# The first gate group of the linear attention by seven products of quarters, and the input's sums written behind the queries' projection

## The chip, the cores and the metric

The kernel runs on one core of a Trainium2 chip. The metric is the device time of one execution in microseconds. Five engines work side by side, each through its own queue in order: TensorE (PE; its weight loads are shown as PEld), VectorE (DVE), ScalarE (ACT), GpSimd (POOL) and SyncE (SP). Weights and activations come from memory by DMA transfers that these queues issue.

## The reference

Two layers. Each normalises the input, projects it, runs three branches beside each other, multiplies each by its own gate path, and sends all of them through one output projection into the residual:

```python
h = _rmsnorm(x, norm_g)
proj = h @ w_in            # 512 tokens x 2048 by 2048 x 7696
(cv_h, cv_b, cv_c, cv_g, sb_q, sb_k, sb_v, sb_g,
 gl_q, gl_k, gl_v, gl_g, gl_lr) = split(proj)
y_conv = short_conv(cv_h, cv_b, cv_c) * silu(cv_g)
y_sb   = stick_breaking(rmsnorm(q), rmsnorm(k), v) * silu(sb_g)
y_gla  = rmsnorm(gla(gl_q, gl_k, gl_v, decay(gl_lr))) * silu(gl_g)
return x + concat(y_conv, y_sb, y_gla) @ w_out
```

The change touches `gl_g`, the gate of the gated linear attention (GLA). It has 512 columns and is projected in two groups of 256, "gla gate 0" and "gla gate 1".

## The kernel before

**Numbers.** Every 32-bit factor is split into a high and a low half of 16 bits. A product is then three matmuls: high by high, high by low, low by high.

**Groups.** The weights are cut into groups of 256 output columns, listed in the order of the work (`spec`). In each layer these are gla v 0, gla v 1, gla q, gla k, gla gate 0, gla gate 1, conv h, c, g and b 0, then four rounds of v, g, q and k of the stick-breaking attention, conv h, c, g and b 1, and eight groups of the output. `weights()` (L536) starts a group: it fetches the group after the next into one of two staging buffers, on POOL's queue, and hooks the preparation of the next group behind a matmul of this one.

**Preparing a group.** ACT squares the two halves of the weights with a running sum (`wmax`, L383). POOL adds these sums over the partitions (L399), and DVE turns the sum into a scale, a power of two (`wscale`, L402 to L417). Then the split: a classic group has ACT write two high halves of 128x2048 (`whi`, L454) and DVE two low halves (`wlo`, L461). They lie in a pool of three pairs of buffers.

**Projecting a group, the classic way.** `project_cols` (L701 to L703) multiplies both halves of the group's columns by all 16 slices of the depth: 2 x 16 x 3 = 96 matmuls with 512 tokens as the moving side.

**Projecting a group by seven products.** Groups named in `QUICK_IN` go through `project_quick`. The matrix product is cut into quarters and made of seven products of quarters instead of eight, by a scheme that shares sums. The weights' part is in `wsums` (L508, L527 to L532): one sum is made by a transfer that POOL issues and that accumulates in place (L386), three by DVE, and seven quarters of 128x1024 are split on ACT (L507) and DVE (L508). They take all three pairs of buffers and one pair more. The input's part is `xsums` (L734, L742): DVE forms sums of quarters of the normalised input once in each layer, and ACT and DVE split them; all the layer's groups in `QUICK_IN` share them as `insums`. The results of the products are combined from PSUM by ACT copies (L808, L812, L815) and five DVE operations (L809 to L821). PSUM has three banks for projections; either way a group takes two.

**What sets the order.** Outside the first stretch, which is ordered by hand, a planner orders each engine's queue: it simulates the program with its own costs and takes, among the instructions that are ready, the one that comes first in the source. Preparation of weights stands ahead of other work (`high_priority`). So the place of a line in the source is its rank, not its time.

**Around the change.** After gla v 0 and v 1 the queries and keys are projected, and each result is scaled: DVE finds the largest value (L1007), POOL reduces it over the partitions (L183), DVE makes a scale of it (L189 to L1014), and ACT copies the result out of PSUM with that scale (L1016). Then `xsums` is called, and the two gates are projected by `project_gate` with a logarithmic sigmoid on ACT and DVE (L874 to L884). DVE and ACT meanwhile prepare the GLA's attention, level by level (L1037 to L1086), whose small matmuls (L1051) fall between the projections.

Of the kernel before, what the change touches and what calls it, by code (L numbers as in the profile page):

```python
# [27 lines left out]


QUICK = ((3, 4, 5, 6), (3, 4, 5, 6))  # L30
QUICK_IN = ("conv c 1", "gla gate 1", "conv g 1", "conv g 0", "conv c 0") + tuple(f"{n} {j}" for n in "gqk" for j in range(4))

AHEAD = (8, 17, 21)

# [9 lines left out]
def hybrid_trunk(ctx, tc, x, norm_g, w_in, conv_w, conv_b, sb_qn_g, sb_kn_g,  # L44
# [33 lines left out]
    def wk(shape, tag, bufs=None, dt=F32):  # L78
        return work.tile(shape, dt, tag=tag, name=nm(tag), bufs=bufs)

    def newbig(tag, shape, dt, side):
        return big.tile(shape, dt, tag=f"big{side}", name=nm(tag))
# [236 lines left out]
    def spec(name, l, src, cols):  # L319
        if name in (QUICK[l] if src is w_out else QUICK_IN):  # L320
            quick.add(len(specs))
        specs.append((l, src, cols))
        names.append(str(name))
# [361 lines left out]
    for l in range(depth):  # L685
# [45 lines left out]
        def sums_of(src, parts, room):  # L731

            def do(f, *a):
                steps.append(f(*a))  # L734

            for t in range(2):
                (h11, h12), (h21, h22), (l11, l12), (l21, l22) = (
                    (a[:, q, 0::2, :], a[:, q, 1::2, :]) for a in src for q in (t, t + 2))

                def put(n, a):  # L740
                    hi, lo = (p_[:, t] for p_ in parts[n])
                    S.activation(hi, a, AF.Copy)  # L742
                    do(V.tensor_tensor, lo, a, hi, ALU.subtract)

                e, g, f = room(t)
                do(V.tensor_tensor, f, h22, l22, ALU.add)
                do(V.tensor_tensor, e, h21, f, ALU.subtract)
                do(V.tensor_tensor, e, e, l21, ALU.add)
                do(V.tensor_tensor, g, h11, e, ALU.subtract)
                do(V.tensor_tensor, g, g, l11, ALU.add)  # L750
                put(0, g)
                do(V.tensor_tensor, f, g, f, ALU.subtract)
                put(3, f)
                put(1, e)
                do(V.tensor_tensor, e, h12, g, ALU.subtract)
                do(V.tensor_tensor, e, e, l12, ALU.add)
                put(2, e)
            return parts
# [11 lines left out]
        def xsums():  # L770

            parts = []
            for _ in range(2):
                a = newbig("s", [P, 4, 2, HK, P], F16, 1 - l)
                parts.extend([a[:, 2 * n], a[:, 2 * n + 1]] for n in range(2))
            return sums_of((xh, xl), parts, lambda t: [wk([P, HK, P], tag) for tag in ("zw", "zw", "g")])
# [73 lines left out]
        def project_gate(mx=None, logistic=False, room=None):  # L850

            g = []

            def dst():
                g.append(room or wk([P, 2, seq], "g"))
                return g[0]

            ps, u = project(True, dst)
            quick_ = bool(g)
            g = dst() if not quick_ else g[0]  # L860
            top = sm(2, "gtop2") if mx is not None else None
            for c in range(2):
                y = g[:, c, :]
                if logistic:
                    a = wk([P, seq], "ga") if quick_ else y
                    tables.append(S.activation(a, ps[c], AF.Sigmoid, scale=u))
                    for b in tables[-9:-1]:
                        order(tables[-1], b)
                    if mx is None:
                        V.scalar_tensor_tensor(y, ps[c], u, a, ALU.mult, ALU.mult)  # L870
                    else:
                        V.tensor_tensor_reduce(y, ps[c], a, u, 0.28, ALU.mult, ALU.max, top[:, c:c + 1])
                    continue
                S.activation(y, ps[c], AF.Copy, scale=u)  # L874
                a = wk([P, seq], "ga")
                S.activation(a, y, AF.Abs)
                S.activation(a, a, AF.Exp, scale=-1.0)
                S.activation(a, a, AF.Ln, bias=1.0)
                V.scalar_tensor_tensor(a, y, 0.0, a, ALU.min, ALU.subtract)
                tables.append(S.activation(a, a, AF.Exp))  # L880
                if mx is None:
                    V.tensor_tensor(y, y, a, ALU.mult)
                else:
                    V.tensor_tensor_reduce(y, y, a, 1.0, 0.28, ALU.mult, ALU.max, top[:, c:c + 1])  # L884
            if mx is not None:
                V.tensor_tensor(mx, top[:, :1], top[:, 1:], ALU.max)
            return g, u
# [114 lines left out]
        for tag in ("qT", "kT"):  # L1002
# [15 lines left out]
            un = sm(1, tag + "un")  # L1018
            V.tensor_tensor(un, p2, u, ALU.mult)
            qku.append(un)  # L1020
        insums = xsums()
        gq, gk = qk
        att_u = sm(1, "attu")
        V.tensor_scalar(att_u, qku[0], qku[1], 0.125, ALU.mult, ALU.mult)
# [30 lines left out]
        for p in range(2):  # L1055
# [53 lines left out]
            for two, bias in ((0, (nT[:, p, 0:1], None, nT[:, p, 2:3], None)),  # L1109
                              (1, (nT01[:, p:p + 1], nT[:, p, 1:2], None, nT[:, p, 2:3]))):  # L1110
                e = wk([P, 2, 256], "e")
                n = [0, 0]
# [201 lines left out]
        for j in range(4):  # L1314
# [14 lines left out]
            g, _ = project_gate(bm[:, 1:2], True)  # L1329
# [144 lines left out]
```

## Time and profile before

| | us |
|---|---|
| median of 3 runs | 1646.34 |
| lowest and highest run | 1645.41, 1650.85 |
| the profiled execution | 1652.09 |
| its span, from the first to the last instruction | 1650.3 |

The profile shows one execution, whose time is 1.8 us more than its span. A row of the timeline begins with the start and the length in us; a row of groups ends with the total, the mean of one in ns, and the idle time of the engine just before, with what ended it. In the first layer gla gate 0 runs on PE from 117.6 to 138.3, gla gate 1 from 138.3 to 158, conv h 0 from 158 to 182, and conv c 0 and conv g 0 from 182 to 224. In the second layer gate 0 begins at 925.1 and gate 1 at 946.5.

### The profile page before, as it was taken

What the parts mean: (1) busy time and instruction counts of PE and PEld (TensorE: products, weight loads), DVE (VectorE), ACT (ScalarE), POOL (GpSimd) and SP (SyncE); (2) the same over time, 40 slices, a digit from 0 to 9 for tenths busy, and PEclk for the clock granted to TensorE, in tenths of its full rate; (3) what the DMA queues carried; (4) which work ended last, traced back from release to release, by engine and by line L of the source; (5) the groups of instructions that cost most, each with busy time, mean ns of one, the idle gap of its engine ahead of it and who ended that gap; (6) DMA issues with size and microseconds to landing.
All of it is one profiled execution on the core that took longest, in us unless ns stands there. A gap on an engine that the chain in (4) does not pass through costs nothing.

```text
span 1650.3 us, 41605 instructions
## 1 busy us (share of the span) xinstructions
PE 1624.0 (98%) x17914; PEld 1342.5 (81%) x17914; DVE 1418.1 (86%) x2377; ACT 1184.7 (72%) x1743; POOL 265.8 (16%) x298
## 2 busy tenths in 40 slices
PE   8999999999999999999999999999999999999999
PEld 6746668989999967799986468689898989668998
DVE  7977989989898978898699689898898889888893
ACT  7667887877777776756766687787777768666571
POOL 0121011111112121111112011221121111211110
PEclk9999999999999999999999999999999999999999
DMA  7144334486768687544633344445776886894441
GB/s 259 54 146 127 73 113 100 116 161 149 166 148 167 148 167 207 161 154 150 204 110 116 103 116 112 132 94 137 152 157 153 151 163 152 165 189 157 154 155 53
DMA packets 193913, 234.90 MB, mean 142 GB/s; under 512 B 90226, under 2 KB 154044, under 8 KB 193216
## 3 DMA queue, kind: packets, MB, share of 16 engines
q0 software_dynamic: 76992, 177.22, 40.5%
q1 hardware_dynamic: 107728, 45.56, 14.5%
q10 hardware_dynamic: 9008, 9.45, 1.7%
q8 instruction: 140, 2.29, 0.6%
q14 instruction: 45, 0.37, 0.1%
HBM read 179.65 MB, written 14.68 MB: 118 GB/s over the span
## 4 chain that ended last, share of the span: by engine, by line
PE 37%; DVE 6%; DMA 4%; ACT 2%; issue 1%; POOL 0%; SPq 0%; DVEq 0%; ACTq 0%; POOLq 0%
PE psp L796 10%; PE psp L793 6%; PE psp L843 5%; PE psp L712 3%; PE psp L714 3%; PE psp L713 3%; PE psp L701 2%; PE psp L702 2%; PE psp L703 2%; DMA st<-in_w_in_dram 2%; DVE wl L508 1%; DMA m<-mixd 1%; DMA th<-za 1%; DVE za L1280 1%; DMA kT<-raw 1%
## 5 line engine op out<-in xcount | busy, mean ns | idle before, releaser
L507 ACT ACTIVATE wh<-st,ws 128x1024 f16<-128x1024 f32 x252 | 280.8, 1145 | 174.5 <-DVE st L527 92.0
L508 DVE SCALAR_TENSOR_TENSOR wl<-st,ws,wh 128x1024 f16<-128x1024 f32 x252 | 316.7, 1278 | 31.1 <-ACT wh L507 31.0
L383 ACT ACTIVATE junk<-st 128x2048 uint8<-128x2048 f32 x150 | 285.4, 1903 | 17.9 <-DMA st<-in_w_in_dram 8.8
L793 PE MATMUL psp<-s,wh 128*128 128x256 f16 x1152 | 195.6, 273 | 0.0
L793 PEld LDWEIGHTS <-wh 128*128 128x128 f16 x1728 | 168.3, 98 | 21.5 <-issue 1.3
L796 PE MATMUL psp<-wh,s 128*128 128x128 f16 x2048 | 176.9, 219 | 1.9 <-issue 1.9
L714 PE MATMUL psp<-wh,m 128*128 128x256 f16 x640 | 174.5, 273 | 1.2 <-DVE m L1189 1.2
L712 PE MATMUL psp<-wh,m 128*128 128x256 f16 x640 | 174.5, 273 | 0.2 <-issue 0.2
L796 PEld LDWEIGHTS <-s 128*128 128x128 f16 x3072 | 172.9, 98 | 2.0 <-issue 2.0
L713 PE MATMUL psp<-wl,m 128*128 128x256 f16 x640 | 174.5, 273 | 0.0
L796 PE MATMUL psp<-wl,s 128*128 128x128 f16 x1024 | 173.2, 219 | 0.0
L461 DVE SCALAR_TENSOR_TENSOR wl<-st,ws,wh 128x2048 f16<-128x2048 f32 x68 | 158.9, 2346 | 14.6 <-ACT wh L454 13.8
L454 ACT ACTIVATE wh<-st,ws 128x2048 f16<-128x2048 f32 x66 | 130.5, 1995 | 40.7 <-DVE ws L415 22.6
L362 POOL DMA_DIRECT2D st<-in_w_in_dram x114 | 109.8, 1029 | 297.8 <-DVE w7l L508 110.7
L793 PE MATMUL psp<-s,wl 128*128 128x256 f16 x576 | 156.7, 273 | 0.0
L796 PEld LDWEIGHTS <-m 128*128 128x128 f16 x2304 | 131.1, 98 | 2.7 <-issue 2.2
L399 POOL PARTITION_ALL_REDUCE wgm<-wm x75 | 55.5, 740 | 482.5 <-ACT junk L383 469.4
L386 POOL DMA_DIRECT2D st<-st x34 | 54.0, 1589 | 307.2 <-ACT junk L383 266.8
L793 PEld LDWEIGHTS <-wl 128*128 128x128 f16 x864 | 84.5, 98 | 13.4 <-issue 3.4
L796 PE MATMUL psp<-wh,m 128*128 128x128 f16 x1024 | 91.5, 219 | 0.4 <-DVE kT L809 0.4
L796 PE MATMUL psp<-wl,m 128*128 128x128 f16 x512 | 87.5, 219 | 0.0
L703 PEld LDWEIGHTS <-wl 128*128 128x128 f16 x448 | 43.8, 98 | 53.6 <-DVE wl L461 2.3
(442 smaller groups left out, 4199.8 us busy)
## 6 DMA issues: line engine op xcount, KB each, us to landing
st<-in_w_in_dram POOLq DMA_DIRECT2D x114, 1024.0 KB, 8.3
st<-in_w_out_dram POOLq DMA_DIRECT2D x32, 1024.0 KB, 8.5
st<-st POOLq DMA_DIRECT2D x34, 512.0 KB, 6.8
st<-in_w_in_dram SPq DMA_DIRECT2D x6, 1024.0 KB, 12.0
mixd<-g POOLq DMA_DIRECT2D x20, 256.0 KB, 7.9
x<-in_x_dram SPq DMA_DIRECT2D x4, 1024.0 KB, 4.9
qT<-in_x_dram ACTq DMA_DIRECT2D x8, 512.0 KB, 6.2
qT<-xs ACTq DMA_DIRECT2D x8, 512.0 KB, 4.0
```

The lines of the kernel that those rows point to most:

```text
L362: load = queue.dma_start(s_, src[l, h * HK * P:(h + 1) * HK * P, c0:c0 + GW].rearrange("(k p) n -> p k n", p=P), max_dma_last_dim=1024)
L383: sq = S.activation(junk(HK * GW).rearrange("p (k n) -> p k n", k=part.shape[1]), part, AF.Square, accum_out=peak[i][:, h:h + 1])
L454: hi = S.activation(wh[:, :, :GW], staged[i][h], AF.Copy, scale=scales[i])
L461: V.scalar_tensor_tensor(wl[:, :, :GW], staged[i][h], scales[i], wh[:, :, :GW], ALU.mult, ALU.subtract)
L507: hi = S.activation(h_, b, AF.Copy, scale=sc)
L508: V.scalar_tensor_tensor(l_, b, sc, h_, ALU.mult, ALU.subtract)
L712: T.matmul(o, ah[:, t, k, :], wh[:, kk, :n], start=st_, stop=False, skip_group_check=True)
L713: T.matmul(o, ah[:, t, k, :], wl[:, kk, :n], start=False, stop=False, skip_group_check=True)
L714: return T.matmul(o, al[:, t, k, :], wh[:, kk, :n], start=False, stop=en, skip_group_check=True)
L793: mm = T.matmul(o, w[q_][:, kk, :], a[p_][:, :, kk, :], start=st_, stop=en, skip_group_check=True)
L796: mm = T.matmul(o[:, t * P:(t + 1) * P], a[p_][:, t, kk, :], w[q_][:, kk, :], start=st_, stop=en, skip_group_check=True)
L843: mm = T.matmul(o[:, :n], a_[:, t, k, :], w[k // HK][part][:, k % HK, :n], start=i == 0 and k == 0, stop=i == 2 and k == KT - 1)
```

## The change

"gla gate 0" joins the groups that are projected by seven products, in both layers. The call of `xsums` moves from behind the loop over queries and keys into it, behind the queries.

```diff
-QUICK_IN = ("conv c 1", "gla gate 1", "conv g 1", "conv g 0", "conv c 0") + tuple(f"{n} {j}" for n in "gqk" for j in range(4))
+QUICK_IN = ("conv c 1", "gla gate 0", "gla gate 1", "conv g 1", "conv g 0", "conv c 0") + tuple(f"{n} {j}" for n in "gqk" for j in range(4))
...
             un = sm(1, tag + "un")
             V.tensor_tensor(un, p2, u, ALU.mult)
             qku.append(un)
-        insums = xsums()
+            if tag == "qT":
+                insums = xsums()
         gq, gk = qk
```

## The prediction

> **What bounds the kernel now.** I read the page first, for the engines' shares.
>
> ```profile
> span 1650.3 us, 41605 instructions
> PE 1624.0 (98%) x17914; PEld 1342.5 (81%) x17914; DVE 1418.1 (86%) x2377; ACT 1184.7 (72%) x1743; POOL 265.8 (16%) x298
> ```
>
> PE is nearly always busy, but ends of matmuls are modelled, so the 98% alone says little. The waits of PE come next; columns are what waited, for whom, the total in us, how often, the longest.
>
> ```profile
> PE psp L793 <- DVE zw L809: 3.1, 2, 1.6
> PE psp L793 <- DVE w7l L508: 2.0, 2, 1.1
> PE psp L703 <- DVE wl L461: 1.3, 1, 1.3
> ```
>
> Only a few microseconds in 1650 are waits for operands. So PE's own stream sets the end, and an instruction taken off it counts in full as long as nobody else becomes late. The three rows show who would: each time DVE, twice in the same place (L809, once in each layer).
>
> Third, the windows, cut at the groups of the GLA stage: first layer's end of q and k (94 to 117), gate 0, gate 1, conv h 0, conv c 0 and conv g 0, conv b 0; then the second layer's k, gate 0, gate 1, conv h 0.
>
> ```profile
> 94.00:117.00 23.00, 23.00 (x108) 10.42 (x107) 18.07 (x45) 18.22 (x23) 3.58 (x5) 1.00 0.28 92
> 117.00:138.00 21.00, 21.00 (x99) 9.53 (x98) 11.74 (x30) 10.53 (x17) 3.36 (x5) 1.00 0.51 126
> 138.00:158.00 20.00, 20.00 (x220) 17.20 (x218) 16.87 (x29) 15.11 (x19) 3.99 (x5) 1.00 0.33 110
> 158.00:182.00 24.00, 23.95 (x228) 11.38 (x225) 21.07 (x48) 20.43 (x41) 2.00 (x2) 1.00 0.44 108
> 182.00:224.00 42.00, 40.38 (x388) 34.56 (x387) 40.98 (x68) 33.27 (x46) 6.28 (x7) 1.00 0.43 113
> 224.00:248.00 24.00, 24.00 (x123) 11.95 (x122) 19.52 (x36) 22.40 (x32) 5.63 (x7) 1.00 0.36 111
> 904.00:925.00 21.00, 21.00 (x99) 9.57 (x98) 14.72 (x35) 16.04 (x21) 2.49 (x4) 1.00 0.31 101
> 925.00:946.00 21.00, 21.00 (x99) 9.52 (x98) 11.51 (x30) 10.32 (x17) 4.11 (x5) 1.00 0.52 126
> 946.00:966.00 20.00, 20.00 (x214) 17.11 (x213) 16.75 (x28) 15.11 (x19) 3.99 (x5) 1.00 0.31 99
> 966.00:990.00 24.00, 24.00 (x244) 11.50 (x235) 21.41 (x49) 20.86 (x41) 1.98 (x2) 1.00 0.46 116
> ```
>
> After the window come its length, then PE, PEld, DVE, ACT and POOL busy, and the granted clock, 1.00 throughout. In gate 0, PE is full while DVE is busy 11.74 of 21 us and ACT 10.53: the group has slack on both. That is the stage the change touches. From 182 to 224 it is the other way round: DVE is busy 40.98 of 42 us, and the first L809 wait lies there.
>
> **PE: seven products for the classic 96 matmuls.** These are the timeline's first and last matmul of gate 0, then gate 1's first, the first of its second product, and the last of its first four products.
>
> ```profile
> 117.58 0.38 PE L701 MATMUL psp<-x,wh 128*128 128x512 f16 x1
> 138.08 0.38 PE L703 MATMUL psp<-x,wl 128*128 128x512 f16 x1
> 138.30 0.27 PE L793 MATMUL psp<-x,wh 128*128 128x256 f16 x1
> 140.92 0.27 PE L793 MATMUL psp<-s,wh 128*128 128x256 f16 x1
> 148.67 0.27 PE L793 MATMUL psp<-s,wh 128*128 128x256 f16 x1
> ```
>
> Gate 0 issues 2 column halves x 16 slices x 3 = 96 matmuls of 512 columns, starting 20.50 us apart over 95 steps: 0.216 each, 20.7 us. The new form has 7 products x 8 slices x 3 = 168 matmuls of 256 columns. Gate 1's first 96 of them start 10.37 us apart over 95 steps: 0.109 each, so 168 take 18.3. PE saves 2.4 us a layer, 4.8 in all.
>
> A rule speaks against this. The Trainium skill, "TensorE: Matmul & The Clock Gate", section "Back-to-back issue gap", gives a sustained spacing of 131 ns for 512 columns and 81 ns for 128. Estimated from that page, 256 columns would take some 98 ns, so 96 wide matmuls 12.6 us and 168 narrow ones 16.4, a loss of 3.8 a layer, or some 1654 us for the kernel. The trace disagrees: it has 216 and 109 ns for these very groups.
>
> **DVE, ACT and POOL: what is added.** The rows are groups by line and form; the number after "busy" is the mean in ns.
>
> ```profile
> L508 DVE SCALAR_TENSOR_TENSOR wl<-st,ws,wh 128x1024 f16<-128x1024 f32 x252 | 316.7, 1278 | 31.1 <-ACT wh L507 31.0
> L507 ACT ACTIVATE wh<-st,ws 128x1024 f16<-128x1024 f32 x252 | 280.8, 1145 | 174.5 <-DVE st L527 92.0 <-PE psp L796 19.4 <-PE psp L714 14.5
> L461 DVE SCALAR_TENSOR_TENSOR wl<-st,ws,wh 128x2048 f16<-128x2048 f32 x68 | 158.9, 2346 | 14.6 <-ACT wh L454 13.8
> L454 ACT ACTIVATE wh<-st,ws 128x2048 f16<-128x2048 f32 x66 | 130.5, 1995 | 40.7 <-DVE ws L415 22.6 <-PE psp L702 9.3 <-PE psp L714 4.2
> L527 DVE TENSOR_TENSOR st<-st 128x1024 f32<-128x1024 f32 x34 | 41.6, 1223 | 0.7
> L816 DVE TENSOR_TENSOR g<-psp,g 128x256 f32<-128x256 f32 x20 | 8.4, 418 | 11.3 <-ACT g L815 11.3
> L808 ACT ACTIVATE g<-psp 128x256 f32<-128x256 f32 x20 | 7.9, 397 | 5.8 <-PE psp L796 5.8
> L386 POOL DMA_DIRECT2D st<-st x34 | 54.0, 1589 | 307.2 <-ACT junk L383 266.8 <-ACT th L1043 20.4 <-ACT own L1103 20.0
> ```
>
> DVE a layer: two low halves go (2 x 2.35 = 4.7); seven low quarters (7 x 1.28 = 8.9), three sums of quarters (3 x 1.22 = 3.7) and five combinations of results (5 x 0.42 = 2.1) come, together +10.0. ACT: 7 x 1.15 + 3 x 0.40 - 2 x 2.00 = +5.2. POOL issues one more accumulating transfer, 1.6 us. The squares stay as many.
>
> What hides it: from 94 to 182 DVE is idle 4.9 + 9.3 + 3.1 + 2.9 = 20.2 us in the first layer (in the second, from 904 to 990, 6.3 + 9.5 + 3.3 + 2.6 = 21.7). Less the 2.4 that PE takes off the stretch, some 18 us stand against 10.0. ACT has at least as much. It fits if at least 10 of the 18 can be used. That is why I take most of the gain, but not all, since two places are tight.
>
> The first lies inside gate 0. Gate 1 today is the precedent: a group of quarters behind a classic one. ACT's and DVE's timelines there:
>
> ```profile
> 132.02 1.15 ACT L507 ACTIVATE wh<-st,ws 128x1024 f16<-128x1024 f32 x1 [5.06 <-PE psp L702]
> 138.81 2.48 DVE L508 SCALAR_TENSOR_TENSOR wl<-st,ws,wh 128x1024 f16<-128x1024 f32 x2 [0.35 <-ACT wh L507]
> ```
>
> The second split waits for the classic group's buffer until 132.02, the sums follow, and the second product's low part is ready halfway through the pair, about 140.1, for a product that starts at 140.92: 0.8 us to spare. In the new gate 0 the same chain runs beside the keys' own scaling:
>
> ```profile
> 117.98 1.63 POOL L386 DMA_DIRECT2D st<-st  x1
> 119.89 0.47 POOL L183 PARTITION_ALL_REDUCE gagm<-gamx  x1
> 121.77 1.25 ACT L1016 ACTIVATE kT<-psp,gas 128x512 f32<-128x512 f32 x2
> ```
>
> The keys' two results leave PSUM from 121.77, so the first bank is free at 122.4; the third product (117.58 + 2 x 2.62 = 122.8) needs it. Before, the second column half (24 x 0.216 = 5.2 later) needed it at the same moment. New splits on DVE and ACT queue around the steps of that chain. One DVE quarter and one sum in front (2.5 us) would cost PE 2.1 us; hidden, nothing. A gain is excluded, since no wait is there today. I take 0.5 a layer, near the precedent, which waits nowhere, and keep 0 to 2.1.
>
> The second is conv c 0, where PE waits 1.6 us for L809 in each layer. If DVE gets there no earlier than now, this wait grows by the 2.4 saved; if its slack carries the extra, not at all. I take 0.5 a layer, nearer to nothing because of the 18 against 10, and keep 0 to 2.4.
>
> **Fetches behind gate 0.** The staging buffer comes free when the seventh quarter is split, about 123 (117.6 plus four DVE quarters or sums of 1.25), not at 116, so conv h 0's weights start some 7 us later.
>
> ```profile
> 116.20 1.78 POOL L362 DMA_DIRECT2D st<-in_w_in_dram  x2 [16.67 <-DVE wl L461]
> 135.24 1.89 ACT L383 ACTIVATE junk<-st 128x2048 uint8<-128x2048 f32 x1
> 157.99 0.39 PE L701 MATMUL psp<-x,wh 128*128 128x512 f16 x1
> ```
>
> Their squares now run at 135.24, and PE needs them at 157.99. That cover of over 20 us hides the delay: nothing. Queued behind that fetch on POOL are the accumulate and the reductions of the rows above. If the order stayed and POOL waited for the buffer at 123, the keys' bank would come 5 us late; the planner sees that release, so I give this to the slower rival.
>
> **The move of the sums.** Their last low parts in either layer:
>
> ```profile
> 84.77 1.22 DVE L734 TENSOR_TENSOR s<-zw,s 128x1024 f16<-128x1024 f32 x1
> 895.22 1.22 DVE L734 TENSOR_TENSOR s<-zw,s 128x1024 f16<-128x1024 f32 x1
> 925.14 0.38 PE L701 MATMUL psp<-m,wh 128*128 128x512 f16 x1
> ```
>
> Sums end at 86.0 and 896.4, before gate 0 begins at 117.6 and 925.1. They already run as early filler, so a source line behind q instead of k moves them at most a little. From the waits, it can at best remove the one L461 wait (1.3) and at worst put two more sums (2.4) ahead of q's low half: I take 0.
>
> **The sum.** 2 x (-2.4 + 0.5 + 0.5) = -2.8. The profiled execution took 1652.09 us with its span of 1650.3, so it would take 1649.3; the runs' median is 1646.34, 5.75 below the profiled one, and becomes 1643.5.
>
> **The rivals.**
>
> *The wait only moves.* PE is early, DVE is not, and conv c 0 takes it back: 2 x (-2.4 + 2.4) = 0, with up to 1.0 inside gate 0: about 1647. For it speaks that both L809 waits already stand there; against it, DVE's idle before. 0.22.
>
> *DVE becomes the bound: slower.* Less than 10 us of its idle can be used, because its splits wait for buffers and the rest for its queue. It decides once over 2.4 us a layer doesn't fit: then conv c 0 waits longer than PE has saved. With half not fitting, 2 x (5.0 - 2.4) = +5.2; with all, 2 x (10.0 - 2.4) = +15.2; POOL's 5 us above gives as much as the first. I put it at 1653. The windows up to 224 speak for it, the idle 4.5 us at 224 to 248 against its going further. The Trainium skill, "Perfetto Trace Analysis", section "Identifying the Most-Contended Engine", takes weight loads and not matmuls for PE's occupancy: by that rule DVE, at 86% against PEld's 81%, is the engine to spare, and this rival holds. The waits of PE speak for the opposite. 0.20.
>
> *The new order also takes waits away.* With both L809 waits (3.1) and the L461 wait gone, and nothing lost: -4.8 - 4.4, 1637. Nothing in the change aims at that. 0.10.
>
> *The change does not do what it says*: gate 0 would still run at L701 to L703. The name is matched as gate 1's is, so 0.01.
>
> **How the numbers follow.** A measurement here can tell about 0.3%, 4.9 us: faster is below 1641.4, slower above 1651.3. The forecast has 0.47; its own range goes from the whole 4.8 kept, 1641.5, to nothing kept, 1646.3. Its lower end touches the border, so that 0.06 of it falls below; with the 0.10 of the rival in which waits go, faster is 0.16. The slower rival lies beyond 1651.3 in nearly all its chance, with a little of the wait that moves: slower 0.22. The rest, 0.62, is the same. Leaving out a tenth at either end gives 1639 to 1654.
>
> **What would show it.** Right: L793 has 336 matmuls more and L701 to L703 192 fewer; gate 0 takes about 18.3 us plus whatever small matmuls fall into it; DVE is 20 us busier in all; L809's waits stay below 5 us. Wrong: PE idle inside gate 0 above 1 us a layer, POOL waiting at L362 in front of the keys' L183, or L809 waits above 7 us. Wrong in the other direction: sums that end elsewhere than before gate 0 with PE waits of other lines gone.

## The result, and the profile after

The changed kernel takes 1649.99 us (median of 21 runs, 1645.96 to 1663.39) against 1646.45 for the kernel before (21 runs, 1645.16 to 1650.85): a ratio of 1.0027, with a 95% interval of 1.0016 to 1.0038. That is 3.5 us slower, where 2.8 us faster was forecast. The profiled execution took 1649.7 us.

The head of the page: span and instructions, then busy time, share and instructions of each engine.

```profile
span 1647.9 us, 41922 instructions
PE 1619.9 (98%) x18058; PEld 1357.2 (82%) x18058; DVE 1434.2 (87%) x2403; ACT 1192.8 (72%) x1759; POOL 273.0 (17%) x300
```

TensorE has 144 matmuls more, as 336 narrow ones in place of 192 wide ones must give. Its time went where the second view shows, the waits of PE:

```profile
PE psp L793 <- DVE g L809: 6.0, 2, 3.0
...
PE psp L796 <- DVE raw L816: 2.8, 2, 1.4
PE psp L793 <- DVE w7l L508: 1.9, 2, 1.1
...
PE psp L703 <- DVE wl L461: 1.3, 1, 1.3
```

The two waits for `zw` in conv c 0 are gone. In their place stand two of 3.0 us for `g` at the same line, now inside gate 0, and two of 1.4 us at L816, in the stick-breaking groups some 200 us later. The windows of gate 0 (first layer), conv c 0 and conv g 0, and gate 0 (second layer) show the price, in PE's column and in the granted clock, the third figure from the end:

```profile
117.00:139.00 22.00, 18.99 (x159) 15.93 (x157) 16.75 (x36) 13.04 (x18) 2.65 (x5) 0.92 0.52 120
...
182.00:224.00 42.00, 42.00 (x395) 35.45 (x394) 38.79 (x62) 34.46 (x45) 7.06 (x8) 1.00 0.38 98
...
925.00:948.00 23.00, 20.01 (x164) 16.39 (x162) 17.83 (x36) 14.12 (x18) 3.73 (x5) 0.93 0.50 115
```

Before, PE was full in gate 0 and lost 1.6 us in conv c 0; now it is the other way round, with 3.0 us lost, and the clock falls as well. PE's timeline around the wait shows both:

```profile
122.63 0.27 PE L793 MATMUL psp<-s,wh 128*128 128x256 f16 x1
125.89 0.37 PE L793 MATMUL psp<-x,wh 128*128 128x256 f16 x1 [2.99 <-DVE g L809]
126.06 0.42 PE L793 MATMUL psp<-x,wl 128*128 128x256 f16 x1
126.27 0.63 PE L793 MATMUL psp<-x,wh 128*128 128x256 f16 x2
126.70 0.42 PE L793 MATMUL psp<-x,wl 128*128 128x256 f16 x1
...
128.82 0.38 PE L793 MATMUL psp<-x,wh 128*128 128x256 f16 x2
129.04 0.27 PE L793 MATMUL psp<-x,wl 128*128 128x256 f16 x1
```

Two products are done at 122.90; the next begins at 125.89, and its matmuls start 0.21 us apart until 128.8, twice the 0.109 they take from then on. What holds it up is in DVE's timeline of the same stretch:

```profile
117.51 0.69 DVE L1007 TENSOR_REDUCE gamx<-psp 128x1 f32<-128x512 f32 x1 [0.41 <-PE psp L703]
118.80 0.16 DVE L1010 TENSOR_TENSOR gam<-gagm 128x1 f32<-128x1 f32 x1 [0.60 <-POOL gagm L183]
118.88 1.28 DVE L508 SCALAR_TENSOR_TENSOR wl<-st,ws,wh 128x1024 f16<-128x1024 f32 x1
120.08 0.15 DVE L189 TENSOR_SCALAR gapc<-gam 128x1 f32<-128x1 f32 x1
120.14 1.27 DVE L508 SCALAR_TENSOR_TENSOR wl<-st,ws,wh 128x1024 f16<-128x1024 f32 x1
121.33 0.14 DVE L190 TENSOR_SCALAR gapc<-gapc 128x1 int32<-128x1 int32 x1
...
121.46 1.28 DVE L508 SCALAR_TENSOR_TENSOR wl<-st,ws,wh 128x1024 f16<-128x1024 f32 x1
122.66 0.15 DVE L191 TENSOR_SCALAR kTp<-gapc 128x1 f32<-128x1 f32 x1
...
122.78 1.28 DVE L508 SCALAR_TENSOR_TENSOR wl<-st,ws,wh 128x1024 f16<-128x1024 f32 x1
123.97 1.22 DVE L532 TENSOR_TENSOR st<-st 128x1024 f32<-128x1024 f32 x1
125.11 0.16 DVE L1014 RECIPROCAL gas<-kTp 128x1 f32<-128x1 f32 x1
...
125.42 0.42 DVE L809 TENSOR_TENSOR g<-psp,g 128x256 f32<-128x256 f32 x1
```

The small rows L1007 to L1014 are the keys' scaling (the keys' chain, below), each step waiting for the one ahead. Between them stand four low quarters and a sum of gate 0's own weights, 4 x 1.28 + 1.22 = 6.3 us. Two of the quarters and the sum serve the fifth and later products, which start no earlier than 127.8 if PE runs on (117.31 + 4 x 2.62). Both ways on for PE are shut by them: the second pair of results needs the keys' bank, which ACT empties only after L1014, and the fifth product, which the planner put third in TensorE's queue, writes on in a bank that L809 must read first.

**The account**, per layer, in the profiled execution: PE saves 2.4. The wait costs 3.0. From its end at 125.89 to 128.80 the clock is at half, so 2.91 us do the work of 1.46 (second layer 2.80 and 1.40). Conv c 0 gives back 1.6, L816 takes 1.4. Together 2 x (-2.4 + 3.0 + 1.4 - 1.6 + 1.4) = +3.6.

This lists prices at five places; that it comes near the 3.5 between the medians proves nothing. The two traces can be laid side by side from a small matmul ahead of the gates (L965) to one of the stick-breaking attention far behind them (L1264, one line lower after the change). The first layer's stretch goes from 85.84 to 370.46 before and from 85.57 to 371.13 after, 0.9 us longer; the second layer's from 893.85 to 1179.17 and from 894.67 to 1180.14, 0.15 longer. So the profiled pair shows a loss of 1.1 us there, not 3.6. Part of the difference is that only the kernel before waits for the keys' transfers in these stretches (L1264, 0.45 and 0.93 us); the rest was not traced. Over the whole span the pair even stands the other way round, 1650.3 before and 1647.9 after, because that execution of the kernel before lost time much later (waits of PE of 1.91 us at 1301.86 and 1.20 at 1488.51). The medians' other 2.4 us no profile shows. Falls of the clock in other runs would account for some of it: the five runs of the changed kernel with a mean clock of 0.999 have a median of 1647.89, 1.4 above that of the kernel before.

### The profile page after: what moved, and what is told of

It is laid out like the page before. It is cut to its first block, busy times and chain, and to the rows that moved or that the text cites. A ratio compares the mean times of both kernels' runs of the same rounds, so it can differ in the third digit from the quotient of the medians.

```text
span 1647.9 us, 41922 instructions
## 1 busy us (share of the span) xinstructions
PE 1619.9 (98%) x18058; PEld 1357.2 (82%) x18058; DVE 1434.2 (87%) x2403; ACT 1192.8 (72%) x1759; POOL 273.0 (17%) x300
## 5 line engine op out<-in xcount | busy, mean ns | idle before, releaser
L507 ACT ACTIVATE wh<-st,ws 128x1024 f16<-128x1024 f32 x264 | 294.6, 1145 | 176.8 <-DVE st L527 90.5
L508 DVE SCALAR_TENSOR_TENSOR wl<-st,ws,wh 128x1024 f16<-128x1024 f32 x264 | 332.8, 1279 | 36.5 <-ACT wh L507 36.2
L793 PE MATMUL psp<-s,wh 128*128 128x256 f16 x1280 | 217.6, 273 | 0.0
L793 PEld LDWEIGHTS <-wh 128*128 128x128 f16 x1920 | 188.8, 98 | 25.5 <-issue 2.7
L793 PE MATMUL psp<-s,wl 128*128 128x256 f16 x640 | 174.3, 273 | 0.0
L461 DVE SCALAR_TENSOR_TENSOR wl<-st,ws,wh 128x2048 f16<-128x2048 f32 x64 | 149.5, 2347 | 12.1 <-ACT wh L454 11.6
L362 POOL DMA_DIRECT2D st<-in_w_in_dram x114 | 112.8, 1081 | 251.9 <-DVE w7l L508 111.1
L454 ACT ACTIVATE wh<-st,ws 128x2048 f16<-128x2048 f32 x62 | 122.4, 1995 | 34.6 <-DVE ws L415 20.2
L399 POOL PARTITION_ALL_REDUCE wgm<-wm x75 | 60.5, 806 | 456.5 <-ACT junk L383 442.6
L796 PEld LDWEIGHTS <-m 128*128 128x128 f16 x2304 | 130.9, 98 | 1.9 <-issue 1.5
L793 PEld LDWEIGHTS <-wl 128*128 128x128 f16 x960 | 94.4, 98 | 19.4 <-issue 7.5
L843 PEld LDWEIGHTS <-m 128*128 128x128 f16 x768 | 75.0, 98 | 12.0 <-issue 1.2
```

Of the source, the lines that this page charges most:

```text
L362: load = queue.dma_start(s_, src[l, h * HK * P:(h + 1) * HK * P, c0:c0 + GW].rearrange("(k p) n -> p k n", p=P), max_dma_last_dim=1024)
L454: hi = S.activation(wh[:, :, :GW], staged[i][h], AF.Copy, scale=scales[i])
L461: V.scalar_tensor_tensor(wl[:, :, :GW], staged[i][h], scales[i], wh[:, :, :GW], ALU.mult, ALU.subtract)
L507: hi = S.activation(h_, b, AF.Copy, scale=sc)
L508: V.scalar_tensor_tensor(l_, b, sc, h_, ALU.mult, ALU.subtract)
L793: mm = T.matmul(o, w[q_][:, kk, :], a[p_][:, :, kk, :], start=st_, stop=en, skip_group_check=True)
```

## The experiments

The theory: it is the place of the new work on VectorE that costs, ahead of the keys' scaling and of L809. Rivals: the moved sums; VectorE's load as such, wherever it stands; and, for the clock, some other cause than idle time. All kernels were timed in turn with the kernel before on the same chip. Where an edit adds lines, those behind it count 2 to 14 higher.

| kernel | median, us (runs) | ratio to before, 95% interval |
|---|---|---|
| gate 0 alone | 1649.18 (12) | 1.0009 [0.9991, 1.0027] |
| moved sums alone | 1647.08 (11) | 0.9997 [0.9981, 1.0013] |
| keys' chain at high priority | 1652.10 (12) | 1.0028 [1.0008, 1.0048] |
| late splits at normal priority | 1665.57 (4) | 1.0108 [1.0076, 1.0140] |
| late splits behind the keys | 1648.97 (12) | 1.0013 [0.9989, 1.0036] |
| half of them behind the keys | 1651.27 (12) | 1.0019 [0.9994, 1.0043] |
| the wait filled with matmuls | 1647.93 (12) | 0.9991 [0.9971, 1.0011] |
| no late low quarters | 1646.83 (12) | 1.0007 [0.9993, 1.0020] |
| the same, late splits behind the keys | 1644.44 (11) | 0.9975 [0.9959, 0.9991] |
| before + 8 passes on VectorE | 1643.78 (9) | 0.9968 [0.9945, 0.9991] |
| before + 2 passes | 1647.35 (11) | 1.0006 [0.9990, 1.0021] |
| late splits behind the keys + 2 passes | 1652.03 (8) | 1.0056 [1.0030, 1.0082] |
| half behind the keys + 2 passes | 1645.31 (11) | 0.9988 [0.9979, 0.9997] |
| half behind the keys + 8 passes | 1654.89 (11) | 1.0052 [1.0033, 1.0072] |

### Which half of the change

Gate 0 alone, the sums in their old place:

```diff
-            if tag == "qT":
-                insums = xsums()
+        insums = xsums()
```

> The kernel before with gate 0 by seven products alone; the sums stay in the source behind the keys. Theory (gate 0's own low quarters and sum on VectorE stand ahead of the keys' scaling and of L809): the time of the changed kernel, about 1650 us or 1.002 to 1.004 of before, with about 6.0 us of PE waits for L809 in gate 0 and a granted clock below 1.00 in the windows of gate 0. Rival (the moved sums delay the keys' chain): about 1641 us, no wait at L809 inside gate 0.

The sums alone:

```diff
-QUICK_IN = ("conv c 1", "gla gate 0", "gla gate 1", "conv g 1", ...
+QUICK_IN = ("conv c 1", "gla gate 1", "conv g 1", ...
```

> The changed kernel with gate 0 classic again, so that only the sums move. Theory: nothing, 1646.4 us, ratio 0.999 to 1.001, waits of PE as before (L809 3.1 us in conv c 0, none inside gate 0). Rival (the moved sums are what costs): about 1650 us, with a new wait in the GLA stage.

Waits of PE with gate 0 alone, then with the moved sums alone:

```profile
PE psp L793 <- DVE g L809: 6.0, 2, 3.0
...
PE psp L796 <- DVE raw L816: 2.8, 2, 1.4
```

```profile
PE psp L793 <- DVE zw L809: 3.0, 2, 1.6
PE psp L793 <- DVE w7l L508: 1.9, 2, 1.1
```

The first has the changed kernel's two pairs of new waits, the second the old pair in conv c 0 and no new one. So gate 0 carries the whole effect, and the moved sums nothing, by the waits and by the second kernel's time. The first kernel's time alone tells less: its runs lie between 1645.7 and 1656.3, and the interval reaches from no change to the lower part of what was expected (1.002 to 1.004). The rival's 1641 us, a ratio of 0.997, lies outside it.

### The clock

The first kernel also shows why its runs differ so. Its two waits of 2.99 us were equal, but the clock fell behind the second only. These windows are cut at the clock's own steps, two around the first wait and two around the second:

```profile
119.82:123.23 3.41, 2.14 (x20) 1.76 (x18) 3.41 (x8) 0.97 (x2) 0.00 (x0) 1.00 0.25 30
123.23:126.65 3.42, 1.70 (x16) 1.53 (x16) 3.20 (x9) 2.36 (x4) 0.00 (x0) 1.00 0.00 0
932.19:935.60 3.41, 0.42 (x5) 0.22 (x4) 3.38 (x12) 1.16 (x2) 0.00 (x0) 1.00 0.00 0
935.60:939.02 3.42, 3.42 (x18) 2.36 (x17) 3.00 (x5) 3.17 (x6) 1.31 (x2) 0.50 0.00 0
```

The first wait is split over two windows, idle 1.27 and 1.72 of 3.41 us: no fall. The second lies in one, idle 2.99: the next window is at half. The changed kernel's own falls followed windows with this much PE:

```profile
121.98:125.39 3.41, 0.92 (x9) 0.68 (x7) 3.41 (x9) 0.55 (x2) 0.00 (x0) 1.00 0.00 0
...
930.93:934.35 3.42, 1.04 (x10) 0.78 (x8) 3.42 (x8) 0.44 (x2) 0.00 (x0) 1.00 0.00 0
```

That is 2.49 and 2.38 idle. So the border lies between 1.72 and 2.38 us idle of 3.41, and where in the window a wait begins decides whether it costs 3.0 or 4.4 us. The two waits can thus make 2.9 us of difference between runs; the changed kernel's runs lie 17 us apart, and no profile shows what else slowed the slowest. The Trainium skill, "TensorE: Matmul & The Clock Gate", section "What's actually happening", has a free-running window of 3413 ns; the trace agrees. The Trainium skill, on the same page, section "Why this matters for your kernels", allows idle gaps up to about 3 us; here a window that was busy for 0.92 to 1.04 us was enough to lose the clock, and the measurement decides.

To part the wait from the clock, 26 matmuls that nobody reads were put into it:

```diff
+            fill = prod(pb, wT2, s_, False)
+            if names[cursor[0] - 1] == "gla gate 0":
+                for n in range(26):
+                    mm = T.matmul(spare, wT2[0][:, n % HK, :], s_[0][:, :, n % HK, :], start=True, stop=True, ...)
+                    order(mm, fill)
+                    fill = mm
...
+            prod(pa, w21, a12, False, after=fill)
```

> The changed kernel with 26 extra matmuls of 128x256 in each gate 0 behind its second product, 26 x 0.109 = 2.8 us, into a PSUM bank that nobody reads: PE computes through the wait for L809 instead of standing idle, and the wait itself stays. Theory (what the idle time costs beyond itself is the granted clock, halved for 3.41 us behind an idle time of some 3 us): clock 1.00 in gate 0 of every run, the single runs within about 2 us of each other as those of the kernel before, 1646 to 1647 us, about 3 us less than the changed kernel although PE does more. Rival (the clock has other causes, and the waiting alone costs the time): runs spread from 1646 to 1660 as with the changed kernel, 1649 to 1650 us.

```profile
117.00:139.00 22.00, 21.83 (x196) 18.88 (x195) 18.11 (x37) 14.45 (x20) 2.91 (x5) 1.00 0.52 121
925.00:948.00 23.00, 22.85 (x184) 17.73 (x183) 19.59 (x41) 15.28 (x19) 4.17 (x5) 1.00 0.43 95
```

PE is full and the clock whole. With 2 x 2.8 us of useless work more, the kernel is not slower than the changed one but, by the two ratios, 0.4% faster. Its highest run says less: it is 1651.41 where the changed kernel's is 1663.39, but the kernel before had one of 1664.24 in the same round. The runs still lie 7 us apart, not 2 as expected: in the profiled one a window at half, from 499.08, followed an unrelated wait of 2.06 us at 496.35. That puts the border between 1.72 and 2.06. Two traces of kernels further down narrow it: a window from 1479.96 with 1.76 us idle kept the clock (half behind the keys + 2 passes), one from 142.86 with 1.87 idle lost it (late splits behind the keys + 2 passes).

### Taking the quarters out of the way

First, rank: the keys' chain, L1007 to L1016, at the high priority that the splits have.

```diff
+            with tc.high_priority() if tag == "kT" else contextlib.nullcontext():
                 mx = sm(2, "gamx")
```

> The changed kernel with the keys' scaling chain traced at high priority, as the splits of gate 0 are. Theory: the keys' banks come free before gate 0's third product, the two waits of 3.0 us for L809 inside gate 0 go, with them the stretch at half clock; 2 x (3.0 + 1.5) = 9.0 us less than the changed kernel, if nothing else becomes late: 1641 us, and not above 1645. Rival (VectorE has too much to do there, so that the wait only goes elsewhere): the idle time of PE in gate 0 and gate 1 stays within 1 us of the changed kernel's, about 1649.

```profile
PE psp L795 <- DVE g L811: 6.0, 2, 3.0
```

This failed: same order on DVE, same wait (L811 is L809 here). The queue as printed above suggests why. Each step of the chain waits for the one ahead, so in the planner's reckoning there is always a moment in which no step of it is ready; a quarter is, and takes 1.28 us. So a rank didn't help this chain of small steps against long pieces that are ready.

Second, the last three splits and the sum are written later, behind the difference L809, at normal priority.

```diff
-        split(b21, 4)
-        V.tensor_tensor(b21, b22, b21, ALU.add)
-        split(b12, 5)
-        split(b21, 6)
+        tails.append(rest)
...
             V.tensor_tensor(y21, zb, y12, ALU.subtract)
+            if tails:
+                tails.pop()()
```

> The changed kernel with the last three splits and the last sum of gate 0's quarters traced behind the difference of its second and third products, so that they are no longer ahead of the keys' scaling and of L809 on VectorE. The work on every engine is the same. Theory: L809's wait inside gate 0 goes from 3.0 us to below 1 a layer, the clock stays 1.00, and the late quarters are asked for only by the fourth and the later products: 1641 to 1645 us. Rival (the load on VectorE as such, wherever it stands): the idle time turns up at the late quarters (L508), as long as before, about 1649.

```profile
PE psp L802 <- DVE wl L508: 10.7, 5, 3.5
```

The wait for L809 is gone, but the late quarters now stand behind sums of the next group and are waited for, with two falls of the clock in each layer. Neither forecast held: 1665.57 us, 19 more than before.

Third, the same pieces stay at high priority and are ordered behind the second of the keys' copies on ACT.

```diff
-                S.activation(o[:, c, :], ps[c], AF.Copy, scale=s_)
+                kcopy = S.activation(o[:, c, :], ps[c], AF.Copy, scale=s_)
+            if tails:
+                with tc.high_priority():
+                    tails.pop()(kcopy)
```

> The changed kernel with the splits of gate 0's fifth to seventh quarter and the sum between them written behind the keys' two copies and ordered behind the second of them, at the same high priority; the work of every engine is the same. Theory (two of four quarters and a sum too early on VectorE hold up the keys' scaling and L809): PE's waits for L809 inside gate 0 fall from 3.0 us to below 0.7 a layer, the granted clock stays 1.00 there, and the time falls by up to 2 x (3.0 + 1.5) = 9.0 us against the changed kernel: 1641 us, up to 1645 if the waits of 1.6 us in conv c 0 come back. Rival (VectorE's load as such): the idle time turns up at the late quarters, about 1649.

And half of it, the fifth quarter left where it was:

```diff
         split(b21, 4)
+        def rest(mm=None):
+            hi = split(b12, 5)
...
+            V.tensor_tensor(b21, b22, b21, ALU.add)
+            split(b21, 6)
```

> Half of that: only the sixth and the seventh quarter and the sum go behind the keys' copies, the fifth stays ahead. Theory: one quarter (1.28 us) fewer stands ahead of L809, since the sum takes the place of the sixth quarter there, so the wait for L809 is 3.0 - 1.3 = 1.7 us a layer, too short for the clock to fall (waits of 1.6 us did not lower it in the kernel before): 2 x (1.3 + 1.5) = 5.6 us less than the changed kernel, about 1644. Rival (VectorE's load as such): as the changed kernel, about 1649.

The first of the two, waits of PE:

```profile
PE psp L804 <- DVE pmix L191: 5.0, 2, 2.5
...
PE psp L804 <- DVE wl L508: 1.3, 2, 0.6
...
PE psp L804 <- DVE g L827: 1.2, 2, 0.6
```

Then the second:

```profile
PE psp L716 <- DVE wl L461: 3.1, 3, 1.3
...
PE psp L806 <- ACT kT L1029: 2.1, 2, 1.1
```

In gate 0 this went as the theory said: 0.6 us and 1.05 us (the keys' copy on ACT, L1029) instead of 3.0. But the kernels were not faster, 1648.97 and 1651.27 us where 1641 and 1644 were expected. In the first kernel a wait of 2.5 us a layer appeared in conv c 0, for one of its low quarters, which ended at 192.91 just ahead of the named L191, and the clock fell with it in both layers (at 192.43 and 1004.81); in the second, 0.9 us at conv h 0's low half and 1.2 at the attention's heads (L1117, first layer). So this part of the theory was too simple, and "load as such" seemed to win.

### Load or place

Two kernels leave out three low quarters a layer, one with the changed kernel's order, one with the late splits behind the keys:

```diff
+            if names[i] == "gla gate 0" and n > 3:
+                parts[n][1] = h_
+                return hi
```

> The changed kernel without the low quarters of gate 0's fifth to seventh quarter (the high part takes their place in the matmuls, so that gate's values are not the reference's): 3 x 1.28 us less on VectorE a layer, the order else as it is, the sum in front of L809 stays. Position theory (what stands ahead of L809 costs) and load theory (VectorE's total in the stage costs) both expect L809's wait inside gate 0 at 3.0 - 2.5 = 0.5 us. Load theory: no new wait behind it either, since 3.8 of the 10.0 us are gone; 1641 to 1643 us.

> The kernel with gate 0's late splits behind the keys' copies, without the low quarters of the fifth to the seventh (that gate's values are not the reference's): same places, 3.8 us less on VectorE a layer. Load theory: the 2.5 us wait in conv c 0 a layer goes, and so does the rest of the gain's loss: 1641 to 1643 us. Position theory (that wait is an accident of the order in which TensorE's products were put): it stays at 2.5 us, 1648 us.

The first, at 1646.83 us and not the 1641 to 1643 of the load theory, still waits 1.7 us at L812, its L809, not the 0.5 both theories expected: the seventh quarter's high part now stands on ACT ahead of the copy that L812 needs (122.71 and 123.77 in ACT's timeline). In the second the 2.5 us in conv c 0 are gone and the kernel is faster than before. That fits load, but the order changed too. The opposite test adds load to the kernel before, and nothing else:

```diff
+            if tag == "kT":
+                with tc.high_priority():
+                    for _ in range(8):
+                        V.scalar_tensor_tensor(wk([P, HK * P], "w7l", 1, dt=F16), o.rearrange(...), 0.5, ...)
```

> The kernel before with eight extra VectorE passes of 128x1024 (8 x 1.28 = 10.2 us a layer) behind the keys' copies, at high priority, whose result nobody reads: the change's load on VectorE without its saving on TensorE and without anything waiting for it. Load theory: VectorE has no room for 10 us between gate 0 and conv g 0; new waits of PE of 2 to 5 us a layer, 1651 to 1657 us. Position theory (only what stands ahead of something due costs): within 1 us a layer of the kernel before, 1646 to 1648 us.

Windows from the end of q to conv b 0 (94 to 248 us), the kernel before and this one (DVE is the third column):

```profile
94.00:248.00 154.00, 152.33 (x1154) 95.05 (x1153) 128.25 (x251) 119.96 (x174) 24.83 (x30) 1.00 0.40 110
```

```profile
94.00:248.00 154.00, 153.69 (x1212) 95.56 (x1211) 141.24 (x277) 119.50 (x177) 25.46 (x28) 1.00 0.40 110
```

VectorE is busy 13 us more in this stretch, and the kernel is 0.3% *faster*: the planner laid out DVE's queue differently, and the waits of 1.6 us for L809 in conv c 0 are gone. This refutes load as such at the size of the change, in the kernel before. It also shows what those waits were; DVE before one of them, in the kernel before:

```profile
191.70 1.22 DVE L532 TENSOR_TENSOR st<-st 128x1024 f32<-128x1024 f32 x1
...
194.31 1.27 DVE L508 SCALAR_TENSOR_TENSOR w7l<-st,ws,w7h 128x1024 f16<-128x1024 f32 x1
...
195.69 0.41 DVE L809 TENSOR_TENSOR zw<-psp,zw 128x256 f32<-128x256 f32 x1
```

A sum and a quarter of conv c 0's own weights stand ahead of a due L809, though they serve its seventh product, which starts at 204.71: the same pattern as in the new gate 0. Three more kernels vary the load, by passes over the keys that nobody reads (1.21 us each):

```diff
+                with tc.high_priority():
+                    for _ in range(2):
+                        V.tensor_reduce(sm(1, "gam"), o.rearrange("p a t -> p (a t)"), AX.X, ALU.max)
```

They are added to the kernel before, to the one with the late splits behind the keys, and to the one with half of them there:

> The kernel before with two such passes a layer instead of eight. Load theory: between the kernel before and something slower, 1647 to 1652 us. Order theory: not slower than before, 1643 to 1647 us, and the 1.6 us waits of conv c 0 are either there as before or gone, not larger by 2.6.

> The kernel with gate 0's late splits behind the keys' copies, with two VectorE passes over the keys more in each layer (128x1024, about 1.28 us each, read by nobody) behind the same copies. Load theory: the wait of 2.5 us in conv c 0 grows with the load, to 4 or 5 us a layer, 1651 to 1654 us. Order theory (the wait belongs to one order of instructions): it changes by something other than the added load and may go; 1643 to 1649 us.

> The kernel with only the sixth and seventh quarter and the sum behind the keys' copies, with the two passes. Load theory: its waits in the stage (1.05 inside gate 0, 0.9 at conv h 0's low half, 1.2 at conv c 0's heads) grow by about 2.6 us a layer, 1653 to 1656 us. Order theory: no more than 1 us a layer above the kernel without the passes, 1643 to 1649 us where no window of half clock falls in.

With two passes in the kernel before, conv c 0 waits as before (1.62 and 1.56), and the time is the same. With the late splits behind the keys, the passes stand ahead of quarters that are due: 1.9 us for the fifth quarter in either layer and again 1.9 for a result (`g`, L827) in the first. That is slower, but the 2.5 us in conv c 0, which load should have made longer, became 0 in the first layer and 0.7 and 0.85 in the second. With half of them behind the keys, all waits in the stage but gate 0's 1.05 are gone:

```profile
117.00:139.00 22.00, 20.94 (x190) 18.23 (x188) 20.99 (x39) 14.90 (x22) 2.63 (x5) 1.00 0.48 105
139.00:159.00 20.00, 20.00 (x252) 16.44 (x249) 20.00 (x36) 19.57 (x31) 3.66 (x3) 1.00 0.39 125
159.00:182.00 23.00, 23.00 (x189) 10.36 (x190) 22.36 (x55) 20.39 (x41) 4.62 (x4) 1.00 0.48 115
182.00:224.00 42.00, 42.00 (x393) 36.55 (x393) 38.30 (x60) 33.48 (x43) 6.96 (x8) 1.00 0.44 117
```

Its ratio of 0.9988 is below the changed kernel's 1.0027 and, at the edge of the intervals, below the 1.0019 of the same kernel without the passes, with *more* work on VectorE. The last kernel has eight passes, with `range(8)`:

> The kernel with the sixth and seventh quarter and the sum behind the keys' copies, with eight VectorE passes a layer (8 x 1.28 = 10.2 us) instead of two. Order theory: the passes stand behind the last wait inside gate 0 and nothing due is behind them for long, so the time stays within 2 us of the kernel with two passes, 1643 to 1647 us. Load theory: with some 20 us more than the kernel before in a stretch in which that kernel had 20 us of idle time, VectorE is full, and the waits come to 4 us a layer or more: 1653 us and above.

```profile
139.00:159.00 20.00, 15.81 (x195) 12.19 (x194) 20.00 (x34) 13.49 (x23) 3.29 (x3) 0.83 0.21 65
```

Its longest waits of PE:

```profile
PE psp L806 <- ACT wh L507: 4.7, 2, 2.8
```

VectorE is full for 20 us on end, PE is not, and the time is 1654.89 us: the order theory's 1643 to 1647 failed, the load theory's 1653 and above held. So the stage has room for at least the 10 + 2 x 1.2 = 12.4 us a layer of the kernel ahead of it, and not for 10 + 8 x 1.2 = 19.6 laid out like this. Whether another order would hold them is not shown: passes stand ahead of two of gate 1's sums (L1034 at 136.16 and 141.15, the sums at 143.62 and 144.75), and on ACT the high quarter that PE waits for (145.78) stands behind squares that waited 1.13 us for a transfer.

The stretches from L965 to L1264 part the stage from the rest of the kernel. They hold the same matmuls in every kernel, but for the 72 more of a gate 0 by seven products and the 26 of the filling. Each figure is from one execution, in us against the kernel before (284.62 and 285.32); the prediction's sum is -1.4 a layer.

| kernel | first layer | second layer |
|---|---|---|
| the changed kernel | +0.9 | +0.2 |
| moved sums alone | 0.0 | -0.1 |
| the wait filled with matmuls | -0.5 | -1.1 |
| late splits behind the keys | +1.5 | +1.6 |
| half of them behind the keys | +0.2 | -1.8 |
| before + 8 passes on VectorE | -1.2 | -1.8 |
| half behind the keys + 2 passes | -2.9 | -3.7 |
| half behind the keys + 8 passes | +4.1 | +2.4 |

With half of the pieces behind the keys and two useless passes, the whole saving arrives in the stage, and conv c 0's old wait is gone on top. The whole kernel shows little of it, 1645.31 us against 1646.35 before in the same round: that execution is 2.4 us slower than the kernel before between the two stretches, with new waits of up to 0.9 us in the stick-breaking groups.

## Why the prediction was wrong, point by point

- **PE's saving, 2.4 us a layer: right.** TensorE has 192 wide matmuls less and 336 narrow ones more, and outside the half clock the narrow ones start 0.109 us apart in the changed kernel too: 41.5 us less and 36.6 more, 4.8 in all.
- **"Inside gate 0 ... I take 0.5 a layer, near the precedent": the step that failed.** The mechanism was named, new splits around the steps of the keys' chain, and sized at "one DVE quarter and one sum in front", 2.1 us at most. Four quarters and a sum stood there, and PE lost 3.0 us a layer, past the 1 us that was to show this wrong. The precedent, gate 1, has no such chain beside it. The planner, which "sees that release", answered by putting the fifth product third, behind L809, which ended at 125.84, hardly sooner than the bank's copy (L1016) began at 126.28.
- **The clock was not in the sum at all.** The waits of before in this stage were up to 1.6 us and left it whole; at 3.0 us it cost 1.4 a layer more, depending on where the wait falls. The filled kernel shows the price: its two stretches are 2.7 us shorter than the changed kernel's, though PE works through the waits; the two falls together are 2.9.
- **Conv c 0, 0 to +2.4, taken 0.5: it was -1.6.** The wait was no measure of VectorE's slack but of the order there, and went with it. A wait of 1.4 us a layer came at L816 instead, a place that the prediction did not look at. In VectorE's timeline two low quarters (319.10 and 320.37) stand right ahead of it, so it looks like the same pattern; that was not tested.
- **DVE's 20 us and the 18 against 10: the balance was right.** The page has 16.1 us more of busy time, in which rows that overlap count once; the groups that change come to about 20. Ten us of idle load cost the kernel before nothing. The slower rival, DVE as the bound, is refuted at this size; at some 20 us a layer the kernel is slower, with load and place not parted. POOL did not hold up the keys either: its reduction L183 ran at 118.37, the fetch L362 at 127.99, 5 us later than the 123 forecast, as the timeline has it.
- **The moved sums, 0: right**, by the kernel that moves them alone.
- **"The wait only moves"** was the nearest rival, with its 1647 us and a loss of 1.1 in the two stretches, but by other places than it named: out of conv c 0, into gate 0 and to L816.

What stays open: why the planner's order loses or keeps a wait some 70 us further on was not traced to a single decision, and 2.4 of the 3.5 us between the medians lie outside what the profiled pair shows. That filling the wait took the whole loss away (ratio 0.9991) points at the waits in gate 0 for them too, but does not show how. That the kernel with half of the pieces behind the keys and two passes is 0.1% faster than the one before is near the edge of what these runs can tell.

## What to carry to other kernels

Where an engine has idle time enough, ask of each new piece of work not only whether it fits but what small, due step it stands ahead of: a chain of 0.15 us steps can take on one long piece at each link. Raising its rank did not help here; ordering the pieces that are needed last behind its end took 2 of the 3 us off the wait, though other waits then kept the kernel from being faster. A wait in a tuned kernel may belong to one order of the queue, so that any edit, a useless one too, can remove it or make it; test the edit's load alone before blaming load.

## What the runs showed of the hardware

The clock's steps all lie on one grid of 3.41 us that runs on through the kernel: in the changed kernel the falls at 125.39 and 934.35 are 808.96 us, or 237 windows, apart. A wait of 3 us therefore has no fixed price. Of the changed kernel's 21 runs those with a mean clock of 0.999 took 1646.14 to 1648.08 us, and those at 0.995 and below 1657.34 to 1663.39. The profiled run, with two falls inside its span, has 0.998, so the slowest must have had more falls than the two waits in gate 0 can make. Single runs of the kernel before were like them in other rounds (1664.24 us at 0.993).
